# Eight of 22 pairs of feed-forward units as seven block products, on one Trainium2 core

## The chip, the core and the metric

The kernel runs on one core of a Trainium2 chip. The time of a run is the time on the device from launch to end, in microseconds (us). The profiler took one execution apart; its span (first to last instruction) is shorter by what lies around it. The compute engines are PE (TensorE, matrix products), DVE (VectorE), ACT (ScalarE) and POOL (GpSimd); SP issues most of the transfers.

## The reference, cut to what matters

One decoder layer (DEPTH = 1) over 512 prompt tokens and 8 samples, handled together as 520 columns. After three mixing branches and a first layer norm, the layer ends in a gated feed-forward part; the change lies there:

```
h  = layer_norm(ALPHA * x + merged @ w_o)          # 1024 channels
u  = causal_dwconv(h @ w_ffn_in, ...)              # 2 x 2816 channels, 3 taps
f  = (silu(u[:D_FF]) * u[D_FF:]) @ w_ffn_out       # gated product, last projection
out = layer_norm(ALPHA * h + f)
```

All is fp32, and the output's precision is held by splitting each operand: `hi` is the value rounded to fp32r, `lo` the rest, and a product is hi·hi + hi·lo + lo·hi.

## The kernel before, in words

Channels lie on partitions, tokens on the free axis. `w_ffn_in` is cut into 44 units of 128 output channels with 1024 inputs (8 blocks of 128), ordered so that units 2i and 2i+1 are the gate and the value part of the same 128 channels: pair i, 22 of them. The 520 columns are two halves of 260 (`HS`, `HB`).

A unit is loaded as one 512 KB transfer into `raw` (two buffers, `wload`, L241), rounded by ACT into `whi` (L161), and DVE writes the rest into `wlo` (L164); `split` does both. Then PE makes 2 halves x 8 blocks x 3 products = 48 matmuls of 128x128 by 128x260 (`mm3`, L357), each half into a PSUM bank of its own (pool `pd`, three banks). ACT copies each half to `fu` and, scaled by the last tap, to `fy` (`ffn_evac`). POOL copies ten columns of `fu` to `nu` (L1465). DVE adds the state of the samples (8 columns) and the two other taps (511 and 510 columns; `ffn_taps`). When both units of a pair are there, ACT applies silu, DVE multiplies, and the product is split at once into `f` hi and lo: ACT rounds 520 columns, DVE subtracts 520. These 44 tiles `f` stay until the last projection (`fo_units`), which has 8 outputs of 22 blocks each, and ends in the second layer norm (`proj_ln`).

The first three pairs (6 units, `early`) run half by half beside the end of the first layer norm. The normed rows `h` stay in eight tiles `r0..r7`, since the second layer norm's input needs ALPHA·h, added on DVE when an output of the projection ends (`head`).

The order of each engine's instructions is set when the program is built: a scheduler walks the instructions by priority, against its own model of their times, and gives tiles their buffers from pools (`t2` 24 buffers, `z2` 18, `l2` 10, `a2` 5). `hp()` puts weights and PSUM reads first; matmuls have the lowest priority and are chained in program order. On the chip each engine then keeps that order. Between its weight loads SP also issues the copies of the caches (`cache_step`).

Of the kernel before, what the change touches and what calls it, by code (L numbers as in the profile page):

```python
# [9 lines left out]
F32 = mybir.dt.float32  # L10
F32R = mybir.dt.float32r
# [105 lines left out]
def build(tc, nc, I, O):  # L117
# [12 lines left out]
    def hp(more=0):  # L130
        return tc.high_priority(HP + more)
# [22 lines left out]
    def fg(name):  # L154
        return pf.tile([128, 512], F32, tag="fg", bufs=PG, name=name)
# [67 lines left out]
    def split(hi, lo, src):  # L223
        act(hi, src)
        return tt(lo, src, hi.bitcast(F32), ALU.subtract)
# [38 lines left out]
    def wunit(src, n, where=None):  # L264
        with hp():
            return wsplit(wload(src, n), n, where)
# [101 lines left out]
    def dense(w, X):  # L368
        ps = dps()
        densemm(ps, w, X)  # L370
        return ps
# [884 lines left out]
    def proj_ln(units, X, nF, nA, nE, gate, nG, wq, wm, res, lg, lb, out, l2):  # L1256
# [154 lines left out]
        else:  # L1411
            for h in range(2):
# [5 lines left out]
                rstd(h)  # L1418
                finish(h, range(8))

    rr = []
    for j in range(8):
        rr.append(rp.tile([128, NT], F32, name=f"r{j}"))
# [36 lines left out]
    XF = []  # L1460
    ft = [t2] * NF + [a2] * NA + [l2] * NL + [z2] * (44 - NF - NL - NA)
    FT = [(ft[i], ft[43 - i]) for i in range(22)]

    def ffn_taps(c, u, y):
        G.tensor_copy(nu[:, c, :], u[:, 510:520])  # L1465
        tt(y[:, 512:520], y[:, 512:520], sfs[:, c, :], ALU.add)
        stt(y[:, 1:512], u[:, 0:511], P('fdw', c * 3 + 1), y[:, 1:512])
        stt(y[:, 2:512], u[:, 0:510], P('fdw', c * 3 + 0), y[:, 2:512])

    def ffn_evac(c, u, y, ps, halves):  # L1470
        with hp():
            for h, p_ in zip(halves, ps):
                act(u[:, HS[h]], p_)
            for h, p_ in zip(halves, ps):
                act(y[:, HS[h]], p_, AF.Identity, scale=P('fdw', c * 3 + 2), bias=P('fdb', c))
# [11 lines left out]
                densemm(ps, w, XH, halves=(h,))  # L1487
            ffn_evac(i // 2 + 22 * (i % 2), u, y, ps, (h,))

    def ffn_chunk(c, i):  # L1490
        if i < NH:
            _, u, y = early[i]
        else:
            u, y = z2("fu"), z2("fy")
            ffn_evac(c, u, y, dense(wunit(I['wfi'][i], 8), XH), (0, 1))
        ffn_taps(c, u, y)
        return y
# [12 lines left out]
    wb = [cp.tile([128, 4, 8, 128], F32R, tag=t, name=f"w{t}") for t in ("xh", "xl")]  # L1510
# [119 lines left out]
```

## Time and profile before

| | |
|---|---|
| median of 3 runs | 1023.53 us (1020.17 to 1026.0) |
| the profiled execution | 1021.31 us |
| its span | 1019.5 us |
| granted clock of TensorE, mean | 0.993 |
| PE, DVE, ACT, POOL busy | 97%, 69%, 49%, 25% of the span |

"Busy" joins overlapping instructions of one engine. Matmuls overlap: one is listed with some 0.28 us, but the next starts 0.12 us after it.

### The profile page before, as it was taken

The page shows a single profiled execution, that of the slowest core. Times are in us where ns is not written, and L with a number is a line of the kernel's source. Part 1 is how long each engine was busy: PE and PEld are TensorE (multiplying, and loading weights), DVE is VectorE, ACT ScalarE, POOL GpSimd, SP SyncE. Part 2 cuts the span into 40 slices and gives each one's busy share as a digit, 9 for nine tenths or more (in the row PEclk, how much of TensorE's full clock was granted, in tenths as well). Part 3 has the DMA queues.
Part 4 walks back from the last instruction along what each step waited for, and adds up shares of the span by engine and source line. Part 5 has one row for each costly group of instructions (what it writes and reads, how often), then busy time and mean ns, then how long its engine had stood idle before and what let it go on. Part 6 is the DMA issues. An engine that isn't in the chain of part 4 may idle for free.

```text
span 1019.5 us, 22101 instructions
## 1 busy us (share of the span) xinstructions
PE 993.4 (97%) x8979; PEld 967.6 (95%) x8979; DVE 705.9 (69%) x1291; ACT 498.1 (49%) x1029; POOL 256.5 (25%) x357
## 2 busy tenths in 40 slices
PE   7999999999999999999999998999999999999994
PEld 7999999999999899989999997999999999999994
DVE  5999899996587579873658888655565655423276
ACT  5255843564453443354553466555555555311144
POOL 0131355363414533321011242111111111001040
PEclk9999999999999999999999998999999999999998
DMA  6553456666526866564346442134334343332322
GB/s 238 192 169 114 139 161 218 208 195 229 195 91 187 244 213 238 159 201 141 120 136 242 151 140 88 53 115 136 118 121 143 116 139 114 113 97 78 96 73 84
DMA packets 48500, 153.06 MB, mean 150 GB/s; under 512 B 9808, under 2 KB 13456, under 8 KB 45328
## 3 DMA queue, kind: packets, MB, share of 16 engines
q1 hardware_dynamic: 35520, 113.15, 33.7%
q0 software_dynamic: 12880, 38.52, 11.8%
q8 instruction: 70, 1.15, 0.5%
q14 instruction: 30, 0.25, 0.1%
HBM read 132.02 MB, written 46.81 MB: 175 GB/s over the span
## 4 chain that ended last, share of the span: by engine, by line
PE 77%; DVE 9%; issue 5%; DMA 4%; ACT 2%; POOL 2%; SPq 0%; POOLq 0%; ACTq 0%
PE ps L357 69%; DVE r L167 2%; DVE wlo L164 1%; DMA kx<-in_kx_dram 1%; DMA raw<-in_wo_dram 1%; DVE wz L164 1%; PE lor L423 1%; PE at L640 1%; POOL rl L761 1%; ACT whi L161 1%; DVE vx L164 1%; DMA swk<-in_swkv_dram 1%; DVE r L164 1%; DMA raw<-in_wrw_dram 1%; DMA xr<-in_xT_dram 0%
## 5 line engine op out<-in xcount | busy, mean ns | idle before, releaser
L357 PE MATMUL ps<-x_hi,whi 128*128 128x260 f32 x1024 | 292.8, 286 | 5.3 <-ACT whi L161 5.2
L357 PE MATMUL ps<-x_hi,wlo 128*128 128x260 f32 x1024 | 293.0, 286 | 1.1 <-DVE wlo L164 1.1
L357 PE MATMUL ps<-x_lo,whi 128*128 128x260 f32 x1024 | 293.6, 287 | 0.3 <-DVE x_lo L164 0.2
L164 DVE TENSOR_TENSOR wlo<-raw,whi 128x1024 fp32r<-128x1024 f32 (+2 forms) x152 | 169.2, 1113 | 175.1 <-ACT whi L161 174.8
L161 ACT ACTIVATE whi<-raw 128x1024 fp32r<-128x1024 f32 (+2 forms) x152 | 146.9, 966 | 221.3 <-PE ps L357 188.1
L357 PEld LDWEIGHTS ps<-x_hi,whi 128*128 128x128 f32 x1024 | 194.2, 190 | 6.8 <-ACT whi L161 5.2
L357 PEld LDWEIGHTS ps<-x_hi,wlo 128*128 128x128 f32 x1024 | 194.5, 190 | 3.1 <-DVE wlo L164 1.7
L357 PEld LDWEIGHTS ps<-x_lo,whi 128*128 128x128 f32 x1024 | 193.8, 189 | 2.0 <-DVE x_lo L164 1.3
L357 PE MATMUL ps<-h_lo,whi 128*128 128x260 f32 x640 | 182.0, 284 | 2.4 <-DVE h_lo L164 2.4
L357 PE MATMUL ps<-h_hi,whi 128*128 128x260 f32 x640 | 181.4, 283 | 0.2 <-DVE r L167 0.2
L357 PE MATMUL ps<-h_hi,wlo 128*128 128x260 f32 x640 | 180.9, 283 | 0.0
L357 PEld LDWEIGHTS ps<-h_lo,whi 128*128 128x128 f32 x640 | 121.0, 189 | 2.7 <-DVE h_lo L164 2.6
L357 PEld LDWEIGHTS ps<-h_hi,wlo 128*128 128x128 f32 x640 | 121.4, 190 | 0.1
L357 PEld LDWEIGHTS ps<-h_hi,whi 128*128 128x128 f32 x640 | 120.8, 189 | 0.4 <-issue 0.4
L357 PE MATMUL ps<-f,whi 128*128 128x260 f32 x592 | 107.7, 283 | 0.0
L1465 POOL COPY nu<-fu 128x10 f32<-128x10 f32 x44 | 40.3, 915 | 217.1 <-ACT fu L161 217.1
L357 PEld LDWEIGHTS ps<-f,whi 128*128 128x128 f32 x592 | 91.5, 188 | 0.1
L167 DVE SCALAR_TENSOR_TENSOR acc<-u,pp,acc 128x511 f32<-128x511 f32 (+29 forms) x120 | 84.3, 733 | 0.4
L357 PE MATMUL ps<-f,wlo 128*128 128x260 f32 x296 | 83.6, 282 | 0.0
L167 DVE SCALAR_TENSOR_TENSOR fy<-fu,pp,fy 128x511 f32<-128x511 f32 x88 | 65.8, 748 | 1.5
L357 PEld LDWEIGHTS ps<-f,wlo 128*128 128x128 f32 x296 | 55.7, 188 | 0.0
L161 ACT ACTIVATE fu<-ps 128x260 f32<-128x260 f32 x88 | 33.0, 378 | 45.3 <-PE ps L357 45.1
(549 smaller groups left out, 1868.9 us busy)
## 6 DMA issues: line engine op xcount, KB each, us to landing
raw<-in_wz_dram SPq DMA_DIRECT2D x63, 512.0 KB, 3.6
raw<-in_wfi_dram SPq DMA_DIRECT2D x44, 512.0 KB, 3.5
out_dram<-in_cc_dram SPq DMA_DIRECT2D x128, 128.0 KB, 3.5
rl<-d POOLq DMA_DIRECT2D x32, 256.0 KB, 4.5
raw<-in_wfo_dram SPq DMA_DIRECT2D x16, 512.0 KB, 3.5
out_dram<-in_cb_dram SPq DMA_DIRECT2D x56, 146.0 KB, 3.7
d<-at POOLq DMA_DIRECT2D x16, 256.0 KB, 3.5
raw<-in_wo_dram SPq DMA_DIRECT2D x8, 512.0 KB, 3.6
```

Of the source, the lines that this page charges most:

```text
L161: return S.activation(out, in_, func, **kw)
L164: return V.tensor_tensor(out, a, b, op=op)
L167: return V.scalar_tensor_tensor(out, a, s, b, op0=op0, op1=op1)
L357: last_mm[0] = T.matmul(ps[i], lhsT=a, rhs=x[:, HS[h]], start=first and k == 0 and q == 0, stop=last and k == len(w) - 1 and q == 2)
L423: T.matmul(ps, lhsT=lor[l][w][:, p, :], rhs=X[x][:, HS[h]], start=i == 0, stop=i == len(wx) - 1)
L640: T.matmul(pst[par][:, c * 128:(c + 1) * 128], lhsT=bk[o:o + 64, c].rearrange("p a b -> p (a b)"), rhs=kr[o:o + 64, c].rearrange("p a b -> ...
L761: LQ.dma_start(x, d[:, :, c * 128:(c + 1) * 128])
L1465: G.tensor_copy(nu[:, c, :], u[:, 510:520])
```

## The change

Eight of the 22 pairs (5, 7, 9, ..., 19) are computed by Strassen's scheme. A pair's product is 256 outputs by 1024 inputs by 520 columns; as two by two blocks (unit by unit, 512 inputs by 512 inputs, 260 by 260 columns) it takes seven block products of 4 x 3 = 12 matmuls in the place of eight. The blocks of h are combined once (`sums_of_input`: four combinations of four blocks each, made on DVE and split into hi and lo), the blocks of the weights for every such pair (four additions on DVE, and seven splits of 512 columns in the place of two of 1024). Sums of products are formed by going on in the same PSUM bank (`A`, then `C_`), with a read of the bank between two steps. The other pairs (`classic`) are computed as before, and the two kinds alternate: while a pair of seven waits for reads and splits, matmuls of a classic pair are put between its block products. Four 256 KB loads stand in the place of two of 512 KB.

For buffers, the eight rows h are written to DRAM (`hd`) and read back before the last projection; their eleven slots (`r2`) hold weights in between. The constants `cst` move to a pool that ends before the feed-forward part. Of the pairs 2 to 21 the gated product stays as one fp32 tile and is split after the last pair (`split_f`), in `l2`, `a2`, `z2` and `t2` as they come free.

```diff
-    cst = cp.tile([128, NCST], F32, name="cst")
+    cst = sp.tile([128, NCST], F32, name="cst", bufs=1)
...
+    def r2(name, shape=(128, NT), dt=F32):
+        return rp.tile(list(shape), dt, tag="r", bufs=11, name=name)
...
-    for i in range(22):
-        yg = ffn_chunk(i, 2 * i)
-        act(yg, yg, AF.Silu)
-        yu = ffn_chunk(22 + i, 2 * i + 1)
-        tt(yg, yg, yu, ALU.mult)
-        hi, lo = [t(f"f{i}", dt=F32R) for t in FT[i]]
-        split(hi, lo, yg)
-        XF.append((hi, lo))
...
+    hd = dr.tile([128, 8, NT], F32, tag="hd", bufs=1, name="hd")
+    for j in range(8):
+        G.dma_start(hd[:, j], rr[j])
+    TT = [l2] * 10 + [a2] * 5 + [r2]
...
+    def sums_of_input():
+        n = 0
+        raw = {}
+        for q in (5, 6, 7, 4):
+            RB[q] = []
+            for k0 in (0, 2):
+                t = raw[q, k0] = t2(f"tr{q}", (128, 2, HB))
+                for i in range(2):
+                    k, d = k0 + i, t[:, i]
+                    b11, b12, b21, b22 = rr[k][:, HS[0]], rr[k][:, HS[1]], rr[k + 4][:, HS[0]], rr[k + 4][:, HS[1]]
+                    if q == 5:
+                        tt(d, b11, b12, ALU.subtract)
...
+                hi, lo = [TT[n + i](f"T{q}", (128, 2, HB), F32R) for i in range(2)]
+                n += 2
+                split(hi, lo, t)
+                RB[q] += [(hi[:, i], lo[:, i]) for i in range(2)]
...
+    def gated(i, ya, yb):
+        act(ya, ya, AF.Silu)
+        raw = ya if i < 2 else t2(f"f{i}")
+        tt(raw, ya, yb, ALU.mult)
+        XF[i] = raw
+        if i < 2:
+            split_f(i, t2)
...
+    def seven(i, odd):
+        bank = fl if odd else fg
+        A, C_, B = [p[:, :HB] for p in (bank("sA"), bank("sC"), fg("sB"))]
+        with hp():
+            raw = [[r2("wr", (128, 4, 128)) for _ in range(2)] for e in range(2)]
+            for e, q in ((0, 0), (1, 0), (1, 1), (0, 1)):
+                ins = nc.sync.dma_start(raw[e][q].rearrange("p k m -> p (k m)"),
+                                        I['wfi'][2 * i + e][:, q * 512:q * 512 + 512])
+            with tc.issue_after(ins.ins):
+                cache_step(2)
+            first = [wp.tile([128, 8, 128], F32R, tag=t, name=t) for t in ("whi", "wlo")]
+            sm = r2("ws", (128, 4, 128))
...
+        w1 = weights(raw[0][0], [x[:, 0:4] for x in first])
+        w5 = weights(added(sm, raw[1][0], raw[1][1]), [x[:, 4:8] for x in first])
+        yield
+        ua, ub = [(t2 if i <= 4 else z2)("fu") for _ in range(2)]
+        block_product(A, w1, RB[1], True, True)
+        copy(ua[:, HS[0]], A)
+        block_product(C_, w5, RB[5], True, True)
+        w6 = weights(added(sm, sm, raw[0][0]))
+        w2 = weights(raw[0][1])
+        yield
+        w7 = weights(added(raw[1][0], raw[1][0], raw[0][0]))
+        w4 = weights(raw[1][1])
+        w3 = weights(added(sm, sm, raw[0][1]))
+        block_product(A, w6, RB[6], False, True)
+        copy(ua[:, HS[1]], A)
+        block_product(B, w2, RB[2], True, True)
+        with hp():
+            tt(ua[:, HS[0]], ua[:, HS[0]], B, ALU.add)
+        yield
+        block_product(A, w7, RB[7], False, True)
+        copy(ub[:, HS[1]], A, scale=-1.0)
+        with hp():
+            stt(ub[:, HS[1]], C_, -1.0, ub[:, HS[1]])
+        yield
+        block_product(A, w4, RB[4], False, True)
+        copy(ub[:, HS[0]], A, scale=-1.0)
+        block_product(C_, w3, RB[3], False, True)
+        with hp():
+            tt(ua[:, HS[1]], ua[:, HS[1]], C_, ALU.add)
+        ys = []
+        for c, u in ((22 + i, ub), (i, ua)):
+            y = z2("fy")
+            with hp():
+                act(y, u, AF.Identity, scale=P('fdw', c * 3 + 2), bias=P('fdb', c))
+            ffn_taps(c, u, y)
+            ys.append(y)
+        gated(i, ys[1], ys[0])
...
     nc.sync.dma_start(O['o_ffn'], nu)
+    for i in range(2, 22):
+        n = 2 * (i - 2)
+        split_f(i, *[r2 if i == 21 else l2 if q < 10 else a2 if q < 15 else z2 if q < 20 else t2 for q in (n, n + 1)])
+    rr = [(r2 if j < 5 else z2)(f"h{j}") for j in range(8)]
+    for j in range(8):
+        G.dma_start(rr[j], hd[:, j])
```

In the steady part the matmuls stand in this order, where S is a pair of seven and C the classic pair after it: products 1 and 5 of S; products 4 and 3 of the S before; the first unit of C (48); products 6 and 2 of S; the second unit of C (48); product 7 of S; then the next group.

## Rows read from the trace of the kernel before

**Rows 1.** The page's first part: busy us (share of the span) and instructions, by engine.

```profile
PE 993.4 (97%) x8979; PEld 967.6 (95%) x8979; DVE 705.9 (69%) x1291; ACT 498.1 (49%) x1029; POOL 256.5 (25%) x357
```

**Rows 2.** The chain that ended last, 560 us to the end: start, length, what.

```profile
623.26 347.38 PE ps L357 x2887
```

**Rows 3.** Busy time by stretch (length, then PE, PEld, DVE, ACT, POOL; clock; DMA).

```profile
100.00:200.00 100.00, 99.69 (x850) 98.71 (x849) 92.85 (x160) 53.82 (x109) 43.23 (x62) 1.00 0.56 184
...
610.00:620.00 10.00, 5.70 (x40) 5.04 (x39) 10.00 (x20) 6.42 (x15) 6.80 (x8) 0.93 0.39 132
620.00:630.00 10.00, 10.00 (x57) 9.27 (x56) 8.76 (x18) 5.28 (x14) 0.52 (x1) 0.72 0.29 93
...
750.00:800.00 50.00, 50.00 (x419) 50.00 (x419) 30.75 (x45) 28.23 (x53) 8.78 (x9) 1.00 0.37 127
```

**Rows 4.** DVE in order of time, one pair: start, us, tile, shape, [idle before <- releaser].

```profile
750.02 1.22 DVE L164 TENSOR_TENSOR wlo<-raw,whi 128x1024 fp32r<-128x1024 f32 x1 [3.00 <-ACT whi L161]
751.17 0.16 DVE L164 TENSOR_TENSOR fy<-fy,sfs 128x8 f32<-128x8 f32 x1
...
752.81 0.70 DVE L164 TENSOR_TENSOR fy<-fy 128x520 f32<-128x520 f32 x1
754.22 0.70 DVE L164 TENSOR_TENSOR f<-fy,f 128x520 fp32r<-128x520 f32 x1 [0.71 <-ACT f L161]
755.78 1.23 DVE L164 TENSOR_TENSOR wlo<-raw,whi 128x1024 fp32r<-128x1024 f32 x1 [0.86 <-ACT whi L161]
...
761.53 1.23 DVE L164 TENSOR_TENSOR wlo<-raw,whi 128x1024 fp32r<-128x1024 f32 x1 [3.00 <-ACT whi L161]
```

**Rows 5.** DVE in order of time around the first layer norm's end, closely queued instructions.

```profile
604.30 0.68 DVE L164 TENSOR_TENSOR wz<-raw,wz 128x512 fp32r<-128x512 f32 x1
604.90 0.43 DVE L164 TENSOR_TENSOR r<-r,cn 128x260 f32<-128x260 f32 x1
...
612.28 0.41 DVE L167 SCALAR_TENSOR_TENSOR r<-r,ps 128x260 f32<-128x260 f32 x1
612.62 0.41 DVE L164 TENSOR_TENSOR r<-r,cn 128x260 f32<-128x260 f32 x1
...
643.59 1.23 DVE L164 TENSOR_TENSOR wlo<-raw,whi 128x1024 fp32r<-128x1024 f32 x1 [7.12 <-ACT whi L161]
...
655.20 0.70 DVE L164 TENSOR_TENSOR fy<-fy 128x520 f32<-128x520 f32 x1
655.82 0.16 DVE L164 TENSOR_TENSOR fy<-fy,sfs 128x8 f32<-128x8 f32 x1
```

**Rows 6.** ACT by group, 700 to 875 us: busy us, mean ns of one, idle before.

```profile
L161 ACT ACTIVATE fy<-ps,pp 128x260 f32<-128x260 f32 x61 | 34.3, 562 | 0.0
L161 ACT ACTIVATE whi<-raw 128x1024 fp32r<-128x1024 f32 x30 | 31.8, 1060 | 24.9 <-PE ps L357 24.9
L161 ACT ACTIVATE fu<-ps 128x260 f32<-128x260 f32 x61 | 23.0, 378 | 38.7 <-PE ps L357 38.7
L161 ACT ACTIVATE fy<-fy 128x520 f32<-128x520 f32 x16 | 10.2, 639 | 0.9 <-ACT fy L161 0.6
```

**Rows 7.** PE in order of time at the last projection's start.

```profile
875.30 0.28 PE L357 MATMUL ps<-h_hi,wlo 128*128 128x260 f32 x1
875.42 0.40 PE L357 MATMUL ps<-f,whi 128*128 128x260 f32 x2
```

**Rows 8.** DVE in order of time: the first use of row h in the last projection.

```profile
889.32 0.42 DVE L167 SCALAR_TENSOR_TENSOR r<-r,ps 128x260 f32<-128x260 f32 x1
```

**Rows 9.** DMA issues: queue, count, KB each, median us to landing.

```profile
raw<-in_wfi_dram SPq DMA_DIRECT2D x44, 512.0 KB, 3.5
...
rl<-d POOLq DMA_DIRECT2D x32, 256.0 KB, 4.5
d<-at POOLq DMA_DIRECT2D x16, 256.0 KB, 3.5
...
r<-in_xT_dram SPq DMA_DIRECT2D x5, 260.0 KB, 5.1
```

More of the change, by code (lines that the diff above doesn't have):

```diff
@@ L1419, in proj_ln @@
                 finish(h, range(8))
+    def r2(name, shape=(128, NT), dt=F32):
+        return rp.tile(list(shape), dt, tag="r", bufs=11, name=name)
     rr = []
     for j in range(8):
-        rr.append(rp.tile([128, NT], F32, name=f"r{j}"))
+        rr.append(r2(f"r{j}"))
         if j in (0, 1, 7):
@@ L1459, in build @@
     G.dma_start(O['o_ffs'], sff)
-    XF = []
-    ft = [t2] * NF + [a2] * NA + [l2] * NL + [z2] * (44 - NF - NL - NA)
-    FT = [(ft[i], ft[43 - i]) for i in range(22)]
+    XF = [None] * 22
     def ffn_taps(c, u, y):
@@ new lines, in block_product @@
+    def block_product(ps, w, X, first, last):
+        with tc.high_priority(-LOW):
+            for k, ((hi, lo), (xh, xl)) in enumerate(zip(w, X)):
+                for q, (a, x) in enumerate(((hi, xh), (hi, xl), (lo, xh))):
+                    with tc.issue_after(last_mm[0].ins):
+                        last_mm[0] = T.matmul(ps, lhsT=a, rhs=x, start=first and k == 0 and q == 0,
+                                              stop=last and k == 3 and q == 2, skip_group_check=not first)
+    def gated(i, ya, yb):
[5 more added lines that the diff above has]
+            split_f(i, t2)
@@ new lines, in split_f, with classic @@
+    def split_f(i, *alloc):
+        hi, lo = [t(f"f{i}", dt=F32R) for t in alloc * (2 // len(alloc))]
+        split(hi, lo, XF[i])
+        XF[i] = (hi, lo)
+    def classic(i):
+        ys = []
+        for e in range(2):
+            c, n = i + 22 * e, 2 * i + e
+            if n < NH:
+                _, u, y = early[n]
+            else:
+                w = wunit(I['wfi'][n], 8)
+                if e == 0:
+                    yield
+                u, y = z2("fu"), z2("fy")
+                ffn_evac(c, u, y, dense(w, XH), (0, 1))
+                if e == 0:
+                    yield
+            ffn_taps(c, u, y)
+            ys.append(y)
+        gated(i, *ys)
@@ new lines, in seven, with weights, added, copy @@
+    def seven(i, odd):
[10 more added lines that the diff above has]
+            sm = r2("ws", (128, 4, 128))
+        def weights(src, where=None, alloc=r2):
+            with hp():
+                hi, lo = where or [t("wz", (128, 4, 128), F32R) for t in (z2, alloc)]
+                last_split[0] = split(hi, lo, src)
+                return [(hi[:, k], lo[:, k]) for k in range(4)]
+        def added(out, a, b):
+            with hp():
+                tt(out, a, b, ALU.add)
+            return out
+        def copy(out, ps, **kw):
+            with hp():
+                act(out, ps, **kw)
+        w1 = weights(raw[0][0], [x[:, 0:4] for x in first])
[16 more added lines that the diff above has]
+            tt(ua[:, HS[0]], ua[:, HS[0]], B, ALU.add)
+        yield
+        block_product(A, w7, RB[7], False, True)
+        copy(ub[:, HS[1]], A, scale=-1.0)
+        with hp():
+            stt(ub[:, HS[1]], C_, -1.0, ub[:, HS[1]])
+        yield
+        block_product(A, w4, RB[4], False, True)
+        copy(ub[:, HS[0]], A, scale=-1.0)
+        block_product(C_, w3, RB[3], False, True)
+        with hp():
+            tt(ua[:, HS[1]], ua[:, HS[1]], C_, ALU.add)
+        ys = []
+        for c, u in ((22 + i, ub), (i, ua)):
+            y = z2("fy")
+            with hp():
+                act(y, u, AF.Identity, scale=P('fdw', c * 3 + 2), bias=P('fdb', c))
+            ffn_taps(c, u, y)
+            ys.append(y)
+        gated(i, ys[1], ys[0])
@@ new lines, in build, with begin @@
+    sums_of_input()
+    for i in range(NH // 2):
+        for _ in classic(i):
+            pass
+    groups, odd, i = [], 0, NH // 2
+    while i < 22:
+        one = two = None
+        if 'CCSCSCSCSCSCSCSCSCC'[i - 3] == 'S':
+            one, odd, i = seven(i, odd), 1 - odd, i + 1
+        if i < 22 and 'CCSCSCSCSCSCSCSCSCC'[i - 3] == 'C':
+            two, i = classic(i), i + 1
+        groups.append((one, two))
+    left, begun = None, set()
+    def begin(n):
+        if n < len(groups) and groups[n][0] and n not in begun:
+            begun.add(n)
+            next(groups[n][0])
@@ new lines, in build @@
+    for n, (one, two) in enumerate(groups):
+        begin(n)
+        if two:
+            next(two)
+        if one:
+            next(one)
+        else:
+            next(two)
+        if left:
+            next(left, None)
+            left = None
+        if one and two:
+            next(two)
+        if one:
+            next(one)
+        if two:
+            next(two, None)
+        begin(n + 1)
+        if one:
+            next(one)
+            left = one
+    if left:
+        next(left, None)
```

16 lines of the change are left out of this document (9 added, 7 removed).

## The prediction

> **What bounds the kernel now.** I read the page's busy shares first, then the chain that ended last, then busy times by stretch, then DVE's instructions in order of time, since DVE gets the new work. Matmuls are busy for 97% of the span [rows 1]. That alone proves nothing, because matmuls overlap in the list. The chain settles it: from 623 to 971 us it is one unbroken piece of 2887 matmuls [rows 2]. In 750 to 800 us PE is busy for all 50 us at clock 1.00, DVE for 30.75 and ACT for 28.23 [rows 3]. So in this part a removed matmul is removed time, as long as the two other engines keep up. The last matmul of the units starts at 875.30 and the first of the last projection at 875.42 [rows 7]: nothing is lost at the border today either.
>
> The sum is made against the profiled execution: 1021.3 us, span 1019.5 and 1.8 around it. It lies 2.2 us under the median of the runs, 1023.5.
>
> **What the change removes.** One classic pair lasts from the weight split at 750.02 to the same split at 761.53 [rows 4]: 11.51 us for 96 matmuls, 0.1199 us each (the two starts of [rows 7] are 0.12 apart). A pair of seven has 7 x 12 = 84 matmuls, 12 fewer: 1.44 us a pair, 11.5 us for eight. That the products accumulate in a bank already written is nothing new: 23 of 24 matmuls of a half do so now. The Trainium skill (TensorE: Matmul & The Clock Gate, "Wait — 56ns, not 53.3ns?") puts warm matmuls at their columns over 2.4 GHz plus some 2.5 ns, which for 260 columns is 0.111 us. By that the 96 matmuls would be worth 10.6 us; the trace has 0.120 here, so I keep 11.5.
>
> **What it adds on DVE.** What counts is how far apart starts of queued instructions lie. 512 columns: 604.30 to 604.90, 0.60. 260 from PSUM: 612.28 to 612.62, 0.34. 520: 655.20 to 655.82, 0.62 [rows 5]. 1024: 750.02 to 751.17, 1.15; the taps of a unit: 751.17 to 752.81, 1.64 [rows 4].
> Pair of seven: 4 additions and 7 splits of 512 (11 x 0.60 = 6.60), 3 reads of PSUM (1.02), taps of two units (3.28), the gated product (0.62): 11.52 us. Classic pair, its last split now moved: 2 x 1.15 + 3.28 + 0.62 = 6.20. Together 17.7 us in a group whose 180 matmuls take 21.58: 82%, against 62% now (30.75 of 50). PE therefore still bounds the group, with 3.9 us to spare. That DVE can be run so full without PE losing is in the trace: in 100 to 200 us it is busy for 92.85 and PE for 99.69 [rows 3].
> The Trainium skill (VectorE: DVE Perf Modes, "The DRAIN you can't avoid") says that the next instruction doesn't start until the pipe of the one before is empty. Taken with the listed durations (0.68, 0.41, 0.70, 1.23 and so on) that makes 19.4 us, 90% of the group, which speaks against this change. Here starts lie some 0.08 nearer than the durations, so I use the starts.
>
> **ACT.** [rows 6], in full durations: 260 columns read 0.378, the same with scale 0.562, 520 silu 0.639, 1024 rounded 1.06. Rounding 512 columns I take at 0.63 by the 520. Pair of seven: 7 x 0.63, 4 reads (1.5), two scaled rows of 520 from SBUF, not shown, between 0.64 and 2 x 0.56 each (I take 0.75, nearer the 520 row), silu: 8.0. Classic: 2.1 + 1.5 + 2.2 + 0.6 = 6.5. 14.5 of 21.58: 67%, not the bound.
>
> **The reads between two products.** Product 6 goes on in bank A only when ACT has read product 1 from it; 5, the products 4 and 3 of the pair before and a classic unit (84 matmuls, 10 us) stand between. 7 after 6: a product and a unit, 7.2 us. 4 after 7: two products, 2.9 us at least, for one ACT read of 0.38. 3 after 5 waits for the DVE read that follows 7: three products, 4.3 us, for 0.34. If the cover were gone, four such reads a pair are 4 x 0.38 = 1.5 us, just the gain of the pair. I count nothing, with 12 us (8 x 1.5) in the rival on queues.
>
> **Weights.** Four 256 KB loads stand for two of 512 KB, which land in 3.5 us [rows 9]. They wait in SP's queue for slots of `r2`, and a classic unit's load queues behind them. Of the 11 slots, three rests of splits (products 7, 4, 3) are held when the next pair wants five; eight are free. A block's split is asked for at least 5.8 us (one classic unit) ahead of its product, and addition, rounding and rest take 0.68 + 0.63 + 0.68 = 2.0. Nothing, as long as DVE's queue is not late.
>
> **Start of the stage.** The sums of the input are 16 instructions of 260 columns and 8 rests of 520 on DVE: 16 x 0.34 + 8 x 0.62 = 10.4 us, and 8 x 0.64 on ACT. The first pair of seven is the sixth, 17 pairs before 875.3: 875.3 - 17 x 11.51 = 680 us. The rows h are ready by 636.5, and DVE then idles 7.12 us to 643.59 [rows 5]. 43 us of room hold 10.4 us of work: 0. The taps of the first units come behind them; if they come too late, `z2` runs out and PE waits: up to 3 us, the 10.4 less the 7.1 idle. The eight stores of h (3.5 us each, as `d<-at` [rows 9]) stand on POOL's queue ahead of its copies to `nu`, for which nobody waits before the end.
>
> **End of the stage.** The 20 splits that are put off cost 20 x 0.62 = 12.4 us of DVE. Their first buffers (`l2`) come free with product 5 of the last pair of seven, 276 matmuls or 33 us before the units end. In those 33 us DVE has the close of the pair before (4.2), 8 weight instructions (4.8), four classic splits (4.6), taps and products of pairs 19 and 20 (4.9 + 3.9) and half of 21 (1.6): 24. So 9 us are left, 14 of the 20 splits. The other six are wanted from the 17th input on, 11.5 us into the projection. At best 0. If none were made early, the first eight inputs are wanted within 2.5 us and take 6 x 0.62 = 3.7, beside 2.4 us of pair 21 and two unit splits of 1.15: up to 6 us. I take 1.
> Row h is first used at 889.32 [rows 8], 13.9 us after the projection starts, and its slots come free before that start. A reload lands in some 4.5 us (`rl<-d` [rows 9]), and the cover holds: 0. Were the slots late by those 13.9 us, the first sum would come one reload late: 4.5, behind which POOL's sums for the norm queue. Also `z2` has three buffers fewer (rows h5 to h7) for the second norm's scratch: 0 to 2 us, taken as 0.
> `cst` moves and `r2` begins where other tiles end: 0, as the five loads of x into r on SP land in 5.1 us and can only move by the like; bounds -1 to +1. Two cache copies a pair for three on average: eight move into the projection, beside loads that wait for nothing; 0.
>
> **Sum.** -11.5 + 1 at the end of the stage + 1 for single waits in eight groups (between 0 and 12) = -9.5. 1021.3 - 9.5 = 1011.8, on the median of the runs 1014.0. The forecast's own range is 1009 to 1018, from -14 (11.5, one from `cst`, and the spread of the runs) to -5.5 (four more of the end's six).
>
> **Rivals.**
> The gain is eaten: waits of 7 to 16 us in all, from the end (up to 6), the start (3) and half a microsecond in each of eight groups (4): 1019 to 1028. For it: four pools are used to the last buffer. Against: the room above in every place.
> DVE's and ACT's queues become the bound. The order is fixed beforehand. If in it DVE stands waiting for each rounding, as it does now for single ones (0.71 before `f`, 0.86 before `wlo` [rows 4]), a group loses 7 x 0.71 + 2 x 0.86 = 6.7 us, and 17.7 + 6.7 = 24.4. That is 1.4 more than the 23.0 of two classic pairs: +11 us, 1034.6 on the median. It bites from 3.9 us of such idleness a group, and the sign turns at 5.3. For it: DVE waits for ACT today before every split of a pair (3.00, 0.71 and 0.86 us [rows 4]), and nothing shows it because DVE has time; the chain addition, rounding, rest crosses the two engines twice, four times a pair. Against: 100 to 200 us [rows 3], where a mixed stream fills 93% of DVE. The Trainium skill (TensorE: Matmul & The Clock Gate, "Architectural detail: the array is 16× 32×32, not 1× 128×128") says that ACT and DVE take their instructions strictly in order, which is what this rival needs.
> A stop of PE has a price beyond itself: after 4.3 idle us in 610 to 620 us the clock in the next 10 us is 0.72 [rows 3], part of them at 1.2 GHz; 10 x 0.28 = 2.8 us more. That is in the upper ends.
> The saving isn't there, since pairs of seven run no faster per matmul: I see no row for it, as shape and operands stay; its time would be 1023 to 1026, part of the middle case.
>
> **Chances.** Forecast 0.62, gain eaten 0.18, queues bound 0.20. The measurement tells about 0.5% (5.1 us) from no change. The forecast lies below -5.1 but for its edge: faster 0.63, same 0.18, slower 0.19. The range to hold 8 of 10: down to 1008, up to the middle case's end, 1029; about 0.04 is left out below and 0.16 above.
>
> **What would show it.** Right: in the profile after, the groups of seven and classic last 21.6 us; DVE is busy for 80 to 90% there; some 96 matmuls fewer; the first matmul of `f` comes some 11 us earlier with at most 2 us of waits behind it. Wrong: PE idle before block products, released by `wlo`, `wz` or ACT's reads (queues); PE idle before `f` (end); clock under 1 in 680 to 880 us. If the units end 11 us earlier and the time doesn't follow, the end of the stage or the second norm took it.

## The result and the profile after

The changed kernel takes 1012.85 us, the median of five runs (1011.33 to 1014.76); the kernel before, run beside it, took 1021.98 (1020.17 to 1026.0). The ratio is 0.9905, interval 0.9878 to 0.9932: faster by 0.9%, with 1014.0 forecast. The profiled execution took 1011.93 us, its span is 1010.1.

The page's busy shares of the kernel after, beside [rows 1]:

```profile
PE 981.3 (97%) x8883; PEld 955.2 (95%) x8883; DVE 754.8 (75%) x1411; ACT 512.0 (51%) x1061; POOL 255.0 (25%) x373
```

There are 8979 - 8883 = 96 matmuls fewer, as counted. DVE has 49 us more work and PE's share stays at 97%. Busy time by stretch of the kernel after, columns as in [rows 3]; all three rows lie where pairs of seven are computed, and the last two are as long as one group (a pair of seven and a classic one):

```profile
750.00:800.00 50.00, 50.00 (x420) 50.00 (x419) 41.06 (x72) 31.34 (x60) 6.99 (x10) 1.00 0.45 146
...
733.00:754.50 21.50, 21.50 (x182) 21.50 (x181) 17.37 (x31) 13.22 (x26) 2.94 (x4) 1.00 0.38 124
754.50:776.00 21.50, 21.50 (x182) 21.50 (x181) 17.39 (x31) 13.29 (x26) 2.95 (x4) 1.00 0.41 137
```

PE is full in every group at clock 1.00, and the matmuls in 50 us are as many as before (420 against 419): their pitch is the old one. DVE went from 30.75 to 41.06 in 50 us and fills 17.4 of 21.5 us, 81%; ACT 13.3, 62%.

DVE in order of time in the kernel after: one group from its classic split to the next, then the end of the units:

```profile
742.82 1.23 DVE L164 TENSOR_TENSOR wlo<-raw,whi 128x1024 fp32r<-128x1024 f32 x1 [3.36 <-ACT whi L161]
...
753.30 1.29 DVE L164 TENSOR_TENSOR wz<-wr,wz 128x512 fp32r<-128x512 f32 x2 [0.59 <-ACT wz L161]
...
764.35 1.23 DVE L164 TENSOR_TENSOR wlo<-raw,whi 128x1024 fp32r<-128x1024 f32 x1 [3.36 <-ACT whi L161]
...
850.50 1.23 DVE L164 TENSOR_TENSOR wlo<-raw,whi 128x1024 fp32r<-128x1024 f32 x1 [3.76 <-ACT whi L161]
...
857.70 1.23 DVE L164 TENSOR_TENSOR wlo<-raw,whi 128x1024 fp32r<-128x1024 f32 x1 [2.40 <-ACT whi L161]
...
869.61 0.70 DVE L164 TENSOR_TENSOR f<-fy 128x520 f32<-128x520 f32 x1
870.22 1.92 DVE L164 TENSOR_TENSOR f<-f,f 128x520 fp32r<-128x520 f32 x3
872.05 0.95 DVE L164 TENSOR_TENSOR wlo<-raw,whi 128x768 fp32r<-128x768 f32 x1
872.92 4.36 DVE L164 TENSOR_TENSOR f<-f,f 128x520 fp32r<-128x520 f32 x7
...
879.87 0.43 DVE L167 SCALAR_TENSOR_TENSOR h<-h,ps 128x260 f32<-128x260 f32 x1
```

A group lasts 764.35 - 742.82 = 21.53 us. DVE's idleness there is one stop of 3.36 us at the classic unit's rounding, where the kernel before has 3.00 [rows 4], and 0.59 at a block's: it is spare time at the end of its list, not seven stops within it. The last two products (869.61 the later one) come after the projection has begun, and ten of the late splits come behind them. PE in order of time, beside [rows 7], shows its beginning and the stop at an `f`:

```profile
865.05 0.28 PE L357 MATMUL ps<-h_hi,wlo 128*128 128x260 f32 x1
865.16 0.41 PE L357 MATMUL ps<-f,whi 128*128 128x260 f32 x2
...
873.68 0.39 PE L357 MATMUL ps<-f,whi 128*128 128x260 f32 x1 [0.31 <-DVE f L164]
```

The border itself loses nothing. PE's list of waits after it (866 us to the end), and for 540 to 562 us (awaited, in total, times, longest), kernel after; between 680 and 866 us the list is empty:

```profile
PE ld L1268 <- DVE h L164: 0.5, 1, 0.5
PE ps L357 <- DVE wxl L164: 0.3, 1, 0.3
PE ps L357 <- DVE f L164: 0.3, 1, 0.3
...
PE ps L357 <- ACT whi L161: 1.3, 2, 0.7
PE ps L357 <- DVE wlo L164: 0.4, 2, 0.2
```

To place the difference I cut both traces at the starts of the same matmuls, counted from the first, and give the lengths of the stages (us). "First on h" is the first matmul of the units, "first on f" the first of the last projection:

```
                                          before    after   difference
5000th matmul to the first on h            96.68    98.07     +1.39
first on h to the start of pair 5          66.97    66.89     -0.08
pairs 5 to 21 (17 pairs, 8 of seven)      195.61   183.79    -11.82
first on f to the 200th after it           24.04    24.84     +0.80
from there to the last matmul             107.29   107.23     -0.06
behind the last matmul                     12.75    12.92     +0.17
```

With +0.26 of the first 5000 matmuls this makes -9.34, but for rounding the difference of the spans. That +0.26 is chance. The kernel after reached its 5000th matmul at 516.4 us here and at 514.8 in its second profile, and the traces of all the runs below lie between 513.8 and 519.2. Part of the scatter is a stretch near 350 us at the clock's lower level (1.2 GHz), which some executions have and others don't (kernel after, then its second profile; the kernel before has 1.00 and 140 matmuls here):

```profile
350.00:360.00 10.00, 9.08 (x106) 8.03 (x102) 2.60 (x5) 4.12 (x11) 2.31 (x4) 0.83 0.62 202
...
350.00:360.00 10.00, 10.00 (x141) 8.87 (x141) 4.58 (x8) 4.97 (x12) 2.02 (x4) 1.00 0.73 234
```

So the stages are what can be compared, and not whole spans to a tenth. The eight pairs gave what their matmuls cost, and two small losses took about 2 us of it back.

### The profile page after: what moved, and what is told of

It is laid out like the page before. It is cut to its first block, busy times and chain, and to the rows that moved or that the text cites. A ratio compares the mean times of both kernels' runs of the same rounds, so it can differ in the third digit from the quotient of the medians.

```text
span 1010.1 us, 22135 instructions
## 1 busy us (share of the span) xinstructions
PE 981.3 (97%) x8883; PEld 955.2 (95%) x8883; DVE 754.8 (75%) x1411; ACT 512.0 (51%) x1061; POOL 255.0 (25%) x373
## 4 chain that ended last, share of the span: by engine, by line
PE 80%; DVE 7%; DMA 4%; issue 4%; ACT 3%; POOL 1%; SPq 0%; ACTq 0%; POOLq 0%
PE ps L357 63%; PE sA L1534 5%; PE sC L1534 2%; DMA raw<-in_wo_dram 1%; PE sB L1534 1%; DVE wlo L164 1%; DVE wz L164 1%; ACT whi L161 1%; PE lor L423 1%; DVE r L167 1%; PE at L640 1%; DVE h L167 1%; DMA kx<-in_kx_dram 1%; PE st L821 1%; DMA rl<-d 1%
## 5 line engine op out<-in xcount | busy, mean ns | idle before, releaser
L164 DVE TENSOR_TENSOR wlo<-raw,whi 128x1024 fp32r<-128x1024 f32 (+2 forms) x136 | 149.4, 1099 | 125.7 <-ACT whi L161 125.5
L161 ACT ACTIVATE whi<-raw 128x1024 fp32r<-128x1024 f32 (+2 forms) x136 | 130.0, 956 | 200.3 <-PE ps L357 170.1
L357 PE MATMUL ps<-h_lo,whi 128*128 128x260 f32 x384 | 109.2, 284 | 2.4 <-DVE h_lo L164 2.4
L357 PE MATMUL ps<-h_hi,whi 128*128 128x260 f32 x384 | 108.7, 283 | 0.2 <-DVE r L167 0.2
L357 PE MATMUL ps<-h_hi,wlo 128*128 128x260 f32 x384 | 108.7, 283 | 0.0
L357 PEld LDWEIGHTS ps<-h_lo,whi 128*128 128x128 f32 x384 | 72.7, 189 | 2.7 <-DVE h_lo L164 2.6
L357 PEld LDWEIGHTS ps<-h_hi,whi 128*128 128x128 f32 x384 | 72.6, 189 | 0.4 <-issue 0.4
L357 PEld LDWEIGHTS ps<-h_hi,wlo 128*128 128x128 f32 x384 | 72.7, 189 | 0.1
L167 DVE SCALAR_TENSOR_TENSOR fy<-fu,pp,fy 128x511 f32<-128x511 f32 (+1 forms) x88 | 65.6, 747 | 0.8
L1534 PE MATMUL sA<-T,wz 128*128 128x260 f32 x288 | 38.5, 283 | 0.0
```

Of the source, the lines that this page charges most:

```text
L357: last_mm[0] = T.matmul(ps[i], lhsT=a, rhs=x[:, HS[h]], start=first and k == 0 and q == 0, stop=last and k == len(w) - 1 and q == 2)
L1534: last_mm[0] = T.matmul(ps, lhsT=a, rhs=x, start=first and k == 0 and q == 0, stop=last and k == 3 and q == 2, skip_group_check=not first)
```

## The experiments

Stage lengths below are cut as in that table, and each run's ratio is against the kernel before on the same chip. The units' stage (pairs 5 to 21) repeats where its program is the same, 183.79 us in five traces; the one from the first matmul on h to pair 5 lies between 66.1 and 67.7 us in all runs. My theory: the gain is the 96 matmuls, DVE has some 4 us to spare in a group, the cover between the reads is needed, and the losses come from the order of the loads and from the late splits. The rivals are in the expectations.

**Placement alone.** The kernel before with the two edits of placement only.

```diff
-    cst = cp.tile([128, NCST], F32, name="cst")
+    cst = sp.tile([128, NCST], F32, name="cst", bufs=1)
...
+    def r2(name, shape=(128, NT), dt=F32):
+        return rp.tile(list(shape), dt, tag="r", bufs=11, name=name)
...
-        rr.append(rp.tile([128, NT], F32, name=f"r{j}"))
+        rr.append(r2(f"r{j}"))
```

> The kernel before with nothing but the two placements of the change: cst in the pool that ends early, and the eight rows r in the eleven r2 slots. Theory (the placement reorders the loads of x, the state and the weights at the end of the branches, and ACT takes the rounding of a weight behind a waiting product): about 1.4 us more than before, and in the trace the first matmul on h comes 1.4 us later after the stretch from 516 us on, with waits of PE on whi near 545 to 560 us, as in the changed kernel. Rival (the 1.4 us are the scatter of one profiled run): the stretch is as long as in the kernel before, time the same as before within 0.5 us.

1023.18 us (ratio 1.0016, 0.9997 to 1.0035). The stage up to the first on h takes 98.41 us, +1.73; the others are those of before (67.24, 195.61, 24.04). The whole time alone would not show it, since the interval holds 1. The placement, taken as nothing in the prediction, costs what the kernel after loses there; which of its two edits does it, this run doesn't part.

**No pair of seven.** All else of the change stays: sums of the input, late splits, reload of h.

```diff
-        if 'CCSCSCSCSCSCSCSCSCC'[i - 3] == 'S':
+        if 'CCCCCCCCCCCCCCCCCCC'[i - 3] == 'S':
...
```

> The changed kernel with all pairs classic: sums of the input, stores and reloads of h and the late splits of f stay, the seven-product pairs go. Theory (the gain is the 96 matmuls): 11.5 us more than the changed kernel, so 1024.4, with 0.8 of it or less lost at the end of the stage as there. Rival 1 (some of the gain came from splitting f late, or from the freed buffers): less than 10 us more. Rival 2 (the seven-product pairs cost waits of their own, hidden in the sum): more than 12.5 us is impossible by that, it would come out under 11.

1024.65 us (1.0031, 1.0009 to 1.0053). The units take 195.61 us again, to the hundredth the time of before: the 11.82 us are the pairs of seven and nothing else. The stage before h (98.23) keeps its loss without them, and the end (24.64) 0.6 of its 0.8 us.

**A ninth pair of seven**, so that the last group has no classic pair behind it.

```diff
-        if 'CCSCSCSCSCSCSCSCSCC'[i - 3] == 'S':
+        if 'CSCSCSCSCSCSCSCSCSC'[i - 3] == 'S':
...
```

> The changed kernel with nine pairs of seven, from pair 4 to pair 20, still alternating. Theory (each pair of seven is worth its 12 matmuls while a classic pair follows): 1.44 us less than the changed kernel, units' end 1.44 us nearer to their start. Rival (DVE at the end of the stage: one classic pair less lies behind the last pair of seven, so more of the late splits are still to be made when the projection starts): PE waits on f grow from 0.8 us by 1.5 us or more and the time is the same or longer.

1015.91 us (0.9942, 0.9923 to 0.9962). From the 6175th matmul, where pair 4 starts, to the first on f it takes 197.19 us, the kernel after 195.29, before 207.12. The ninth pair adds 1.90 instead of taking 1.44, and the end goes from 24.84 to 26.02. Of the 1.90, some 0.8 come from beginning with pair 4, as the run further down with all pairs one place earlier shows (196.05 for 195.29). PE in order of time at its last block products:

```profile
863.24 1.70 PE L1534 MATMUL sA<-T,wz 128*128 128x260 f32 x12 [1.65 <-ACT fu L161]
...
865.40 0.39 PE L1534 MATMUL sC<-h_hi,wz 128*128 128x260 f32 x1 [0.46 <-DVE fu L167]
```

Product 4 waits for ACT's read of product 7, product 3 for DVE's read behind it: where nothing classic is left to put between, this pair of seven costs more than it saves.

**More work on DVE.** Instructions that change no value, behind each unit's taps: four, so eight a pair.

```diff
             ffn_taps(c, u, y)
+            for _ in range(4):
+                tt(y, y, y, ALU.max)
```

> The changed kernel with eight more DVE instructions in each pair of seven (y = max(y, y) over 520 columns, which changes nothing), 8 x 0.62 = 5.0 us a group. Theory (a group has 3.9 us of DVE time to spare and can use all of it): DVE needs 17.7 + 5.0 = 22.7 us a group against 21.5 of PE: 1.2 us a group, 9 to 10 us in all, 1022.5, and PE waits inside the groups for splits or reads. Rival (the spare time lies in gaps that ACT's roundings leave and can't be used): most of the 5.0 us a group shows, 25 to 40 us, 1038 to 1053. Second rival (the extra work is put off behind the weights and only piles up at the end of the stage): PE has no wait inside the groups and all of the loss lies before f.

1020.6 us (0.9995, 0.9973 to 1.0018): the gain is gone. But not where the theory had put it. Busy time by stretch, then PE's waits from 680 us on, of this kernel:

```profile
797.50:819.00 21.50, 21.50 (x182) 21.50 (x182) 21.50 (x39) 13.19 (x25) 6.23 (x4) 1.00 0.37 123
...
872.00:882.00 10.00, 5.44 (x23) 4.85 (x24) 9.30 (x16) 6.14 (x11) 0.00 (x0) 0.66 0.46 179
```

```profile
PE ps L357 <- ACT f L161: 5.9, 1, 5.9
...
PE ps L357 <- DVE f L164: 1.0, 2, 0.8
```

DVE is full and PE is too, with all its 182 matmuls: the units take 183.67 us, no more than in the kernel after. DVE's work on the gated products falls behind instead (a gated product starts 21 us after its pair's last block product at first and 34 at the seventh of the eight, where the kernel after has 9 and 13), and the debt falls due at the border: the stretch behind it goes from 24.84 to 33.77 us. Part of that is the stop itself, part the granted clock of 0.66 after it. The second rival had it so: no wait inside the groups, all of the loss before `f`.

**Half of that**, two behind each unit's taps.

```diff
             ffn_taps(c, u, y)
+            for _ in range(2):
+                tt(y, y, y, ALU.max)
```

> The changed kernel with four more DVE instructions in each pair of seven (y = max(y, y) over 520 columns, which changes nothing), 4 x 0.62 = 2.5 us a group. With eight more, PE had no wait inside the groups and all of the loss, 9.7 us, lay before f: DVE's backlog of 8 x 1.2 us. Theory (DVE's spare 3.9 us a group is all usable, and only what exceeds it piles up): 17.7 + 2.5 = 20.2 of 21.5 us a group, no backlog, PE without waits in the groups; but in the last 33 us, where the late splits are made, three closes of pairs lie, 2 to 3 us less for the splits: 1 to 3 us more than the changed kernel, all before f. Rival (the loss goes with the added work from the first instruction): half of the loss of eight, 4 to 5 us.

1017.31 us (0.9953, 0.9934 to 0.9972). DVE fills 19.6 of 21.5 us, the units take 183.77, and the end 28.52, +3.7. That lies between what the theory (1 to 3) and the rival (4 to 5) gave and decides for neither alone. But no backlog grows: a gated product starts 14 us behind its last block product in every group up to the sixth. The waits on `f` come to 2.0 us, and the granted clock is 0.83 from 872 to 882 us. So DVE's spare time in the groups is not free even while it lasts; that the late splits are what needs it is my reading, as they are what PE waits for.

**No cover.** The block products of a pair follow one another, the classic units come behind them.

```diff
         if one:
             next(one)
-        else:
+            next(one)
+            next(one)
+            next(one, None)
+        if two:
             next(two)
-        if left:
-            next(left, None)
-            left = None
-        if one and two:
-            next(two)
-        if one:
-            next(one)
-        if two:
             next(two, None)
         begin(n + 1)
-        if one:
-            next(one)
-            left = one
```

> The changed kernel with the seven products of a pair one behind the other (1, 5, 6, 2, 7, 4, 3) and the classic pair's 96 matmuls behind them, in the place of the mixed order. Theory (the classic units cover the reads of PSUM between two products on a bank): reads now lie in the open, PE waits before products 4 and 3 for ACT's and DVE's reads, as it did for 1.8 and 0.6 us at the last of nine pairs; 2.4 to 4 us a pair, 19 to 32 us in all, most of it released by fu. As my prediction priced it, four reads of 0.38, it would be at most 12 us. Rival (what the order covers is the DVE work on the weights, 11.5 us of it in a stretch of 10.1 us of matmuls): PE waits for wz and wlo, not for fu, and the loss is 1.4 us a pair or more, from 11 us.

1031.21 us (1.0085, 1.0061 to 1.011), the units 201.25 us, +17.5. Busy time by stretch of one group and of the last one, then PE's longest waits from 680 us on:

```profile
754.50:776.00 21.50, 20.50 (x169) 20.08 (x168) 17.44 (x30) 12.65 (x25) 2.74 (x4) 1.00 0.41 136
...
840.50:862.00 21.50, 17.39 (x137) 16.73 (x137) 17.16 (x30) 15.18 (x29) 2.10 (x3) 0.99 0.22 74
```

```profile
PE sA L1534 <- ACT fu L161: 4.8, 8, 1.4
PE sA L1534 <- DVE wz L164: 4.1, 8, 0.5
PE sC L1534 <- DVE fu L167: 2.2, 1, 2.2
```

A group starts 13 matmuls fewer in its 21.5 us, 13 x 0.12 = 1.56 us. The last one loses 45, 5.4 us. Seven times 1.56 and 5.4 make 16.3 of the 17.5; in the 10 us behind them the granted clock is 0.86 and 75 matmuls start in the place of some 83, about 1 us more. Each group has two stops of some 0.5 us in the list, one for weights (`wz`) and one for ACT's read (`fu`), and the last one adds 1.4 and 2.2 for reads: the classic units cover both. The theory's 19 to 32 us, nearly all for reads, were too much; the rival, weights and 11 us or more, has the size, but only a part of the cause.

**The order of the loads.** In the kernel after, SP issues the load of `sff` ahead of loads of x into the rows r. Here it goes behind the last of these (`last_r`), as in the kernel before.

```diff
-            nc.sync.dma_start(rr[j + 1], I['xT'][:, j + 1, :])
+            last_r[0] = nc.sync.dma_start(rr[j + 1], I['xT'][:, j + 1, :])
...
-    nc.sync.dma_start(sff, I['sffn'])
+    with tc.issue_after(last_r[0].ins):
+        nc.sync.dma_start(sff, I['sffn'])
```

> The changed kernel with the load of the samples' state (sff) put behind the loads of x on SP, as it stands in the kernel before; by that ACT rounds a weight before the product m2 again. Theory (the changed placement costs by that order): the stretch from the 5000th matmul to the first on h is again 96.7 us long where the changed kernel has 98.1; 1.4 us less than the changed kernel, 1011.4. Rival (it is another thing of the placement, as the loads' landing times or where the tiles lie, or scatter): 98 us, time as the changed kernel's.

1009.41 us (0.988, 0.986 to 0.990). The stage before h takes 96.11 us. ACT in order of time in the kernel after, the same place in the kernel before, then in this one, with this one's PE waits for 540 to 562 us:

```profile
547.02 0.64 ACT L161 ACTIVATE m1h<-gt 128x520 fp32r<-128x520 f32 x1 [0.57 <-DVE gt L164]
...
549.85 0.64 ACT L161 ACTIVATE m2h<-gt 128x520 fp32r<-128x520 f32 x1 [2.19 <-DVE gt L164]
...
551.41 0.63 ACT L161 ACTIVATE whi<-raw 128x512 fp32r<-128x512 f32 x1 [0.92 <-PE ps L357]
```

```profile
550.03 0.63 ACT L161 ACTIVATE whi<-raw 128x512 fp32r<-128x512 f32 x1 [2.61 <-DMA raw<-in_wrw_dram]
550.57 0.62 ACT L161 ACTIVATE m2h<-gt 128x520 fp32r<-128x520 f32 x1
```

```profile
545.39 0.64 ACT L161 ACTIVATE m1h<-gt 128x520 fp32r<-128x520 f32 x1 [0.64 <-DVE gt L164]
...
548.53 0.63 ACT L161 ACTIVATE whi<-raw 128x512 fp32r<-128x512 f32 x1 [2.49 <-PE ps L357]
549.07 0.62 ACT L161 ACTIVATE m2h<-gt 128x520 fp32r<-128x520 f32 x1
```

```profile
PE ps L357 <- DVE wlo L164: 0.6, 1, 0.6
```

In the kernel after, the rounding of weights `whi` stands on ACT behind the rounding `m2h`, which waits 2.19 us for DVE; PE then waits 1.3 us for `whi`. With the load moved, `whi` goes first and those 1.3 us are gone from the list. One edit in the order of issue turned round the order of two ACT instructions that it doesn't touch. Over all runs the stage parts the two orders: 98.07 to 99.18 us in the eight traces with the changed placement and the load not moved, 96.11 to 97.48 in the five with the load moved (96.68 before). With the placement alone, SP issues `sff` at 540.99 us, ahead of x (543.80) as in the kernel after; why the placement draws it forward, no run shows. The next stage, up to pair 5, took 67.70 us here, 0.8 more than in the kernel after and the longest of all runs, so one whole time shows less than the stage.

**The kernel after once more**, unchanged, beside it.

> The changed kernel once more, beside the one with the other load order. Both theories: 1012.9 within 1 us; the stretch from the 5000th matmul to the first on h 98.1 us if it is fixed by the program's order, 96.5 to 98.5 if it is scatter.

1011.01 us (0.9894, 0.9873 to 0.9914); stages 98.37, 66.67, 183.79, 24.84, 107.22. The loss before h and that at the end repeat; the difference to the run before it in whole times, 1.6 us, is inside the two intervals, so it is the stages that show it.

The last four runs look for the 0.8 us at the end; all have the load order of the run above.

**Four rests on GpSimd**, to take the splits of inputs 13, 15, 17 and 19 off DVE (the lo part only).

```diff
-        split(hi, lo, XF[i])
+        if i in (13, 15, 17, 19):
+            act(hi, XF[i])
+            G.tensor_tensor(lo, XF[i], hi.bitcast(F32), op=ALU.subtract)
+        else:
+            split(hi, lo, XF[i])
```

> The kernel with the other load order, and of the late splits four rests (f13, f15, f17, f19) computed by POOL in the place of DVE. In the changed kernel 200 matmuls of the last projection take 24.84 us where they took 24.04 before: PE waits for f at the 67th. Theory (DVE's queue of late splits is what the end waits for): four of them less are 2.5 us less DVE time there; the 200 matmuls take 24.0 us, 0.8 us less in all, 1008.6. Rival (the buffers that the splits wait for, or ACT's roundings, set it): 24.8 as before. Second rival: POOL needs 1.5 us for each by its 0.75 for 260 columns, and PE waits for POOL instead: more than 24.8.

1011.76 us (0.9904, 0.9875 to 0.9933); the end takes 27.62 us, 2.8 longer. PE's waits there:

```profile
PE ps L357 <- DVE f L164: 0.7, 1, 0.7
PE ps L357 <- POOL f L1552: 0.5, 1, 0.5
```

The run doesn't decide whether DVE's work is what is late, because DVE's time did not fall. DVE instructions that run at the same time as one of these rests are longer: taps take 1.79 us instead of 0.74, and four late splits 4.74, where seven take 4.36 in the kernel after. From the orders of time of POOL and DVE in this run:

```profile
864.65 1.37 POOL L1552 TENSOR_TENSOR f<-f,f 128x520 fp32r<-128x520 f32 x1 [1.09 <-ACT f L161]
864.78 1.79 DVE L167 SCALAR_TENSOR_TENSOR fy<-fu,pp,fy 128x510 f32<-128x510 f32 x1
...
869.62 4.74 DVE L164 TENSOR_TENSOR f<-f,f 128x520 fp32r<-128x520 f32 x4
869.85 3.35 POOL L1552 TENSOR_TENSOR f<-f,f 128x520 fp32r<-128x520 f32 x2 [1.21 <-ACT f L161]
```

That costs DVE some 3 us, more than the four rests of 0.62 that it was spared, and PE waits for POOL too, as the second rival had it; the granted clock is 0.67 from 870 to 875 us.

**The pairs of seven one place earlier**, so that three classic pairs follow the last of them.

```diff
-        if 'CCSCSCSCSCSCSCSCSCC'[i - 3] == 'S':
+        if 'CSCSCSCSCSCSCSCSCCC'[i - 3] == 'S':
...
```

> The kernel with the other load order, and the eight pairs of seven one pair earlier: 4, 6, ..., 18, with three classic pairs behind the last. Theory (the end loses 0.8 us because the buffers and DVE's time for the late splits come only 33 us before the projection): one classic pair more, 11.5 us, behind the last pair of seven, so the 200 matmuls take 24.0 us: 0.8 us less. Against it stands the wait of 0.4 us that PE had near 691 us when a pair of seven was the fifth. Net 0 to 0.8 us less, 1008.6 to 1009.4. Rival (the end loses because the gated products of the last pairs come late whatever lies before): 24.8, and with the wait at the start 0.5 us more.

1011.77 us (0.9898, 0.9866 to 0.993). The end takes 24.63 us, as with no pair of seven at all (24.64): the time behind the last block product is worth 0.2 of the 0.8 us, not more. In the kernel after, in that with no pair of seven and in this one DVE makes the same ten splits behind the last product, three and then seven, although with no pair of seven it is busy for only 82 of 150 us from 700 us on. So DVE's amount of work is not what is late. The units take 184.56 us, 0.77 more, with a wait of 0.4 for ACT at the first pair of seven.

**The last product in place.** It takes no tile of `t2`, so no request of a split stands behind its request.

```diff
-        raw = ya if i < 2 else t2(f"f{i}")
+        raw = ya if i < 2 or i == 21 else t2(f"f{i}")
```

> The kernel with the other load order, and the last pair's gated product left in its fy tile, as those of pairs 0 and 1 are, in the place of a 24th t2 tile. In every kernel so far with late splits PE stops at the same place, the 67th matmul of the last projection, the first on f14, however much time lies behind the last pair of seven. Theory (buffers: f10 to f20 go to t2, whose requests stand in line behind that of the last gated product, so these splits are all made behind it): now they can be made before it, and the first 200 matmuls take 24.0 us in the place of 24.84; 0.8 us less in all, 1008.6. Rival (DVE's amount of work at the end): 24.8.

1010.6 us (0.9878, 0.9857 to 0.9899). The end takes 23.98 us, the 24.04 of before, and PE's wait for `f` has left the list; the whole time doesn't part it from the load order alone. DVE in order of time in this kernel (product of pair 19, then splits; its times lie about 1.7 us before those of the kernel after), then ACT's roundings here and in the kernel after:

```profile
866.55 0.69 DVE L164 TENSOR_TENSOR f<-fy 128x520 f32<-128x520 f32 x1
867.16 0.69 DVE L164 TENSOR_TENSOR f<-f,f 128x520 fp32r<-128x520 f32 x1
...
868.43 1.92 DVE L164 TENSOR_TENSOR f<-f,f 128x520 fp32r<-128x520 f32 x3
...
865.79 2.74 ACT L161 ACTIVATE f<-f 128x520 fp32r<-128x520 f32 x5
```

```profile
867.46 1.16 ACT L161 ACTIVATE f<-f 128x520 fp32r<-128x520 f32 x2
870.34 0.64 ACT L161 ACTIVATE f<-f 128x520 fp32r<-128x520 f32 x1 [1.72 <-DVE f L164]
```

A split goes at once behind the product of pair 19, and four in all lie before the last product (870.26 here); in the kernel after the rest of the last unit's taps and the last product (869.61) come first, and ACT stands for 1.72 us until that product is done. What doesn't change is the ten splits before, nor DVE's stops of 3.76 and 2.40 us between them.

**Both together**: pairs of seven one earlier and the last product in place.

```diff
-        raw = ya if i < 2 else t2(f"f{i}")
+        raw = ya if i < 2 or i == 21 else t2(f"f{i}")
...
-        if 'CCSCSCSCSCSCSCSCSCC'[i - 3] == 'S':
+        if 'CSCSCSCSCSCSCSCSCCC'[i - 3] == 'S':
...
```

> Both: the pairs of seven one pair earlier (4 to 18), and the last gated product in place. Theory (buffers): 24.0 us for the first 200 matmuls here too, against 24.63 with the pairs earlier alone; the wait of 0.4 us near the first pair of seven stays, so 0.4 us behind the kernel with the product in place alone. Rival (DVE's work): 24.6, as with the pairs earlier alone.

1009.12 us (0.9862, 0.9847 to 0.9877), with the end at 24.0 us and the units at 184.59: the fastest of these versions against the kernel before. From the run before it the interval doesn't part it, nor from the load order alone. The stage before h took 97.48 us here, about 1 us above the other four with the load moved.

## Why the prediction was right

**The matmuls.** -11.5 forecast, -11.82 measured in the stage, and all of it goes when the pairs of seven are taken out. That is 0.123 us a matmul, near the trace's pitch of 0.120. The Trainium skill (TensorE: Matmul & The Clock Gate, "Wait — 56ns, not 53.3ns?") would have made it 10.6, by estimate; no run here comes near that, and the measurement decides.

**DVE and ACT in the group.** 17.7 of 21.58 us forecast for DVE, 17.4 of 21.5 measured; ACT 14.5 against 13.3. To add up starts instead of durations was right: the Trainium skill (VectorE: DVE Perf Modes, "The DRAIN you can't avoid"), read with listed durations, gave 19.4 (the rows make it 19.2), a fill that the group reaches only with four instructions more (19.6). The two scaled rows of ACT, taken at 0.75, took 0.824 (ACT groups, 700 to 850 us, kernel after):

```profile
L161 ACT ACTIVATE fy<-fu,pp 128x520 f32<-128x520 f32 x14 | 11.5, 824 | 7.9 <-DVE fu L164 7.4
```

The rival of queues needed 3.9 us a group of DVE standing before roundings of the blocks; it stood 0.59. That DVE's spare time runs out at some 4 us was right, though: with eight instructions more (5.0 us) the kernel was back at the time of before. What the rival and the experiment's theory both had wrong is the place. The gated products had room to come later, so PE was not stopped in the groups but at the border, once.

**Single waits in groups.** +1 forecast, 0 measured: the term was too big by 1.

**The reads and their cover.** Nothing forecast, nothing seen; without cover 1.56 us a group, where 1.5 was priced. That the two agree is luck: the price was for four reads, and in a group only about half of the loss is reads, the rest weights. The 12 us of the prediction left out the last group and the weights; 17.5 were measured.

**Start.** The sums of the input cost nothing that shows above that stage's scatter, as forecast: 66.89 us against 66.97.

**Placement.** Taken at 0 within -1 and +1, it costs 1.4 us in the profiled runs (1.7 alone): mis-sized, and outside its bounds. I priced the loads' landing, not the order of issue that goes with it and the turned order on ACT.

**End of the stage.** +1 forecast, +0.80 measured, but the way there was wrong. I reckoned 14 of 20 splits before the end from DVE's spare time. Ten were made by then, the tenth as the projection began, and ten came after the last product (3 at 870.22, 7 at 872.92), although DVE stood idle for 3.76 and 2.40 us shortly before. Reading the code, I take it that requests for tiles of one name are served in their order, so that a split asks for its tile only once the last product has had its own; the run with that product in place, which takes away the loss and brings four splits before it, fits this, as no count of DVE's work does. That the order of requests is the cause rests on this edit alone, which also moves the product to another tile; a run that changes only the order was not made. Nor does it explain why the spare time gave fewer splits than reckoned: the two idle stops are as long with the product in place, and why no split is made in them stays open.

**Reload and the rest.** First use of h in the projection at 879.87, 14.7 us after its start (13.9 in [rows 8]), without a wait. The DMA issues of the kernel after (queue, count, KB each, us to landing):

```profile
wr<-in_wfi_dram SPq DMA_DIRECT2D x32, 256.0 KB, 4.4
...
hd<-r POOLq DMA_DIRECT2D x8, 260.0 KB, 2.3
h<-hd POOLq DMA_DIRECT2D x8, 260.0 KB, 5.7
```

Reloads land in 5.7 us against 4.5 estimated from `rl`, the stores in 2.3 against 3.5; 14.7 us covers both.

So three small terms were off by -1, +1.4 and -0.2 and the large one by -0.3, and they all but cancel: -9.4 in the spans for -9.5 forecast. The mechanism was right, but that the sum came within 0.1 us is luck, the more so as the first 5000 matmuls scatter by more than a microsecond; the second profile of the kernel after lies 10.9 us under that of the kernel before. The middle case, a gain eaten by waits, had one place right (the end, at 0.8 of up to 6 us). Its start meant the sums of the input, which cost nothing; the loss before h is the placement, for which it had no term.

## What to carry to other kernels

In a stage that PE bounds, price a removed matmul at its pitch in the trace and the added DVE work by the starts of queued instructions, then ask how much of DVE's spare time is already promised to something else: here the late splits. Work that may come late did not stop PE where it was added here; it ran up a debt that fell due at the next place where PE needs its result. Edits that look free, a tile moved to another pool or a load issued earlier, can turn round instructions on other engines, as here on ACT: compare the order of issue there as well.

## What the runs showed that I had not expected

- DVE can be full for whole groups (21.50 of 21.50 us) with PE starting all its 182 matmuls.
- After the stop of 5.9 us at the border, the next matmuls start 0.215 us apart instead of 0.12 (the clock's lower level of 1.2 GHz, granted clock 0.66 over those 10 us). Of the 8.9 us that the end loses, about two are this (8.9 less the waits of 5.9 and 1.0); the waits are the rest.
- The classic units covered not only the reads but, in nearly the same measure within a group, the preparation of block weights (without them a stop of some 0.5 us for each).
- DVE instructions that ran beside POOL's `tensor_tensor` took up to 1.79 us where they take 0.74 elsewhere: work moved from DVE to POOL was not DVE time saved.
- The four loads of 256 KB of a pair of seven land in 4.4 us each, the 512 KB of a classic unit in 3.5 [rows 9]: half the bytes, no less time.
